# Turning the probabilities of the banded heads: four TensorE transposes into PSUM, or one transposing DMA per pair inside SBUF

## The chip, the cores and the metric

The kernel runs on one core of a Trainium2 chip. The metric is the device time of one execution in microseconds; three executions of the kernel before were timed and their median is used. A separate execution was profiled, and every row shown below comes from that one.

## What is computed

One decoder layer for 2048 tokens of width 1024. The input is normalised and projected once; the projection feeds two attention mixers of eight heads each (head width 64). Mixer A, "FoX", is causal attention with a cumulative forget-gate bias. Mixer B is a banded attention: each query sees itself and the 127 keys before it, plus one learned logit per head (the sink) in the softmax. Both outputs are gated, concatenated, projected out, normalised and added to the input. The change is in mixer B:

```python
def sliding_window_sink_attention(q, k, v, sinks):        # blocks of 128 queries
    ...
    s = jnp.einsum('bnqhgd,bnshd->bnhgqs', qb, kk, ...) * (d ** -0.5)   # keys: previous block and own block
    ...
    s = jnp.where(mask[None, :, None, None], s, -jnp.inf)               # the band of 128 keys
    sink = jnp.broadcast_to(sinks..., s.shape[:-1] + (1,))
    p = jax.nn.softmax(jnp.concatenate([s, sink], axis=-1), axis=-1)[..., :-1]
    out = jnp.einsum('bnhgqs,bnshd->bnqhgd', p.astype(vv.dtype), vv)
    return out.reshape(B, S, SWA_Q_HEADS * d)
```

## The kernel before

The layer runs in four stages: a prologue (conditioning vectors, the first weights, the normalised input turned to `hT`), the banded stage, the FoX stage and the output projection. Numbers that need more than half precision are kept as two 16-bit parts, a high one and the rest ("high" and "low"), and every product is made of three matmuls: high by high, high by low, low by high.

**The banded stage** is a list of 32 windows. Window n does the parts of one *pair*: two blocks of 128 queries times two heads, so four 128x128 probability tiles with queries on partitions. The matrix work of other projections (`proj_units`, `value_units`, lines L351 and L369) is cut into units and poured between these parts by `fill`, so that TensorE always has something to do. A pair goes through these steps, each a method of the class `Pair`:

- `scores` (L889): twelve matmuls into one PSUM tile `pss`, at the end of the window before its own.
- `maxima` (L896 to L904), VectorE: the band mask is written into `pss`, the sink logit into one column, the row maximum is taken, and L904 makes the bias `b_nb` of the exponential.
- `exps` (L911), ScalarE: four exponentials from `pss` to `sm_` in SBUF, 32-bit, with their row sums in `b_rs`.
- `turn` (L914 on), one window later: TensorE transposes the four tiles of `sm_` into the PSUM tile `pxb` (L918). A step later ScalarE copies `pxb` to 16 bits (`fold[:, 0]`, L927), VectorE subtracts that copy from `pxb` (`fold[:, 1]`, L928) and takes the reciprocal of the row sums (L930), and GpSimd cuts the band's two triangles out of `fold` with four affine selects (L932, L934) into `ptb`. There is one buffer `fold`.
- `pv` (L946), another window later: 24 matmuls of `ptb` with the values, then VectorE scales (L952), and `o_store` (L285 to L295) splits the result and stores it to DRAM `o_d`.

**What sets the order.** The program is recorded in the order in which each engine then runs; nothing is reordered. `after(n, f)` puts a function off by n ticks, and `tick` runs those that are due. A window holds four ticks, one for each quarter of its filling units:

```python
            tick()
            if n:
                wd.maxima()
            fill(part[0])
            if n:
                windows[n - 1].turn()
            tick()
            if n:
                wd.exps()
            fill(part[1])
            tick()
            if n > 1:
                windows[n - 2].pv()
```

after which follow `fill(part[2])`, `tick()`, `fill(part[3])`, the `scores` of the next window, and one load of `w_out` rows for a sum of squares (`wsq`, L1183 and L1179).

**Other users of the same queues in this stage.** SyncE's DMA queue issues the four quarter copies `qs<-qf` of each rotary projection (L751), which VectorE reads five ticks later (L764, L765) and whose end is L768 and L758, and the `wsq` loads. GpSimd issues, in its own order between the selects, weight loads (L221), the gate path's stores (L394), the stores to `o_d`, and for each weight a column of 128 maxima written to DRAM (`mx_d`, L230, 4 bytes a row) and read back as a row (`mxr`, L235), on which VectorE waits before it scales that weight (L246 to L253). PSUM has three banks `bk` for the filling units; a bank is free again when ScalarE and VectorE have read it (L749 and L754, L396 and L392, L375 and L379).

In the output stage, from 981 us on, `load` reads `o_d` with DMAs that transpose on the way (L1483, 128 rows of 1024 16-bit numbers each). They are the only transposing DMAs of the kernel before.

Of the kernel before, what the change touches and what calls it, by code (L numbers as in the profile page):

```python
# [10 lines left out]
F32 = mybir.dt.float32  # L11
F16 = mybir.dt.float16
# [3 lines left out]
AF = mybir.ActivationFunctionType  # L16
ALU = mybir.AluOpType
AX = mybir.AxisListType

P = 128  # L20
# [4 lines left out]
CH = 512  # L25
# [18 lines left out]
def hybrid_layer(  # L44
# [17 lines left out]
    V, A, G, PE, SP = nc.vector, nc.scalar, nc.gpsimd, nc.tensor, nc.sync  # L62
# [5 lines left out]
    PSUM = bass.MemoryType.PSUM  # L68
# [14 lines left out]
    def sm(n, tag):  # L83
        return small.tile([P, n], F32, tag=tag, name=tag)
# [71 lines left out]
    ident = const.tile([P, P], F32, name="ident")  # L156
# [45 lines left out]
    def after(n, f):  # L202
        late.append([n, f])

    def tick():
        now = [f for n, f in late if n <= 1]
        late[:] = [[n - 1, f] for n, f in late if n > 1]
        for f in now:
            f()
# [221 lines left out]
    def turn(ci, k, px=None):  # L431

        px = px or ps_x.tile([P, CH], F32, tag="x", name="px")
        for u in range(4):
            PE.transpose(px[:, u * P:(u + 1) * P], xt[ci * 4 + u][:, k * P:(k + 1) * P], ident[:])
        hf = hst.tile([P, CH], F32, tag="hf", name="hf")
        hi, lo = hT[ci][:, 0, k, :], hT[ci][:, 1, k, :]

        def scaled():
            for dst in ([hi] if k % 2 == 0 else []) + [hf[:]]:  # L440
                A.activation(dst, px[:], AF.Identity, scale=Gp[:, k:k + 1], bias=Shp[:, k:k + 1])

        def split():
            if k % 2:
                V.tensor_copy(hi, hf[:])
            V.tensor_tensor(lo, hf[:], hi, op=ALU.subtract)

        return scaled, split

    def turn_x(ci, k):  # L450
        scaled, split = turn(ci, k)
        after(1, scaled)
        after(2, split)
# [10 lines left out]
    st = start.enter_context(tc.tile_pool(name="start", bufs=1, reuse_waits="tile"))  # L464
    wad = start.enter_context(tc.tile_pool(name="wad", bufs=8, reuse_waits="tile"))
    with tc.manual_schedule():
# [172 lines left out]
        w_low("kb", 0, 1)  # L639
        w_low("vb", 0, 1)  # L640
        turned = [turn(0, k) for k in range(5)]
        squares(1)
        shf0 = col8("shf0")
# [9 lines left out]

        PE.transpose(bk[0][0:1, 0:P], bmx[:], ident[:])
        turned += [turn(0, k, bk[k - 4]) for k in (5, 6)]
        bm = st.tile([1, 1], F32, name="bm")
        V.tensor_reduce(bm[:], bk[0][0:1, 0:P], axis=AX.X, op=ALU.max)
# [66 lines left out]
    def swa_pool(name, bufs, **kw):  # L724
        return swa.enter_context(tc.tile_pool(name=name, bufs=bufs, reuse_waits="tile", **kw))
# [3 lines left out]
    stp = swa_pool("stp", 2)  # L729
# [143 lines left out]
    class Pair:  # L873
# [32 lines left out]
        def exps(self):  # L906
# [3 lines left out]
            for n in range(4):  # L910
                A.activation(self.sm_[:, n], self.s4[:, n // 2, n % 2], AF.Exp, scale=scl[key][:],  # L911
                             bias=self.nb[:, n:n + 1], accum_out=self.rs[:, n:n + 1])

        def turn(self):  # L914

            px = ps_t.tile([P, 4, P], F32, tag="t", name="pxb")
            for n in range(4):
                PE.transpose(px[:, n, :], self.sm_[:, n, 1:P + 1], ident[:])  # L918
            even = (8 * self.j + self.i // 2) % 2 == 0
            self.ptt = [ptp.tile([P, 2, 4, P], F16, tag=f"pt{b}", name="ptb") if even else  # L920
                        stp.tile([P, 2, CH], F16, tag="st", name="ptb") for b in range(2)]
            ptt = [t[:].rearrange("p a (n c) -> p a n c", n=4) if not even else t[:] for t in self.ptt]
            self.ptt = ptt
            fold = ptp.tile([P, 2, 4, P], F16, tag="fo", name="fold")

            def split():
                A.activation(fold[:, 0], px[:], AF.Copy)  # L927
                V.tensor_tensor(fold[:, 1], px[:], fold[:, 0], op=ALU.subtract)  # L928
                self.rinv = sm(4, "b_ri")
                V.reciprocal(self.rinv[:], self.rs[:])  # L930
                for n in range(2):
                    G.affine_select(ptt[0][:, n], fold[:, n], [[0, 4], [-1, P]], ALU.is_ge, 0.0,  # L932
                                    base=-1, channel_multiplier=1)
                    G.affine_select(ptt[1][:, n], fold[:, n], [[0, 4], [1, P]], ALU.is_ge, 0.0,  # L934
                                    base=0, channel_multiplier=-1)

            after(1, split)

        def pv(self):
            j, i = self.j, self.i  # L940
# [178 lines left out]
    def fill(n, each=None):  # L1119

        for _ in range(n):
            for f in events.pop(pos[0], []):
                f()
            punits[pos[0]]()
            pos[0] += 1
            if each:
                each()
# [9 lines left out]
    with swa_order:  # L1137
        fill(N_PRO - 4, tick2)
        psx.close()
        sws = swa_pool("sws", 2)  # L1140
        ptp = swa_pool("ptp", 1)
        ps_s = swa_pool("ps_s", 1, space=PSUM)
        ps_t = swa_pool("ps_t", 1, space=PSUM)
        ps_pv = swa_pool("ps_pv", 1, space=PSUM)
        wsp = swa_pool("wsp", 2)
        wss, wst = sm(16, "a_m"), sm(2, "wst")
        wsq = {}
        base = N_PRO
        NW = len(windows)
        windows[0].scores()  # L1150
        windows[0].maxima()
        fill(2, tick2)
        windows[0].exps()
        fill(2, tick2)
        for n, wd in enumerate(windows):
            goal = base + (N_SWA - base) * (n + 1) // NW
            todo = goal - pos[0]
            part = [todo * (m + 1) // 4 - todo * m // 4 for m in range(4)]
# [13 lines that stand above are left out]
            fill(part[2])  # L1172
            tick()
            fill(part[3])
            if n + 1 < NW:
                windows[n + 1].scores()

            if n:
                A.activation(wsq[n - 1][:], wsq[n - 1][:], AF.Square, accum_out=wss[:, (n - 1) % 16:(n - 1) % 16 + 1])  # L1179
            if n == 16:  # L1180
                V.tensor_reduce(wst[:, 0:1], wss[:], axis=AX.X, op=ALU.add)
            wsq[n] = wsp.tile([P, 2 * P], F32, tag="wsq", name="wsq")
            SP.dma_start(wsq[n][:], w_out0[n // 4 * P:(n // 4 + 1) * P, n % 4 * 2 * P:(n % 4 + 1) * 2 * P])  # L1183
        tick()
        fill(5)
        windows[NW - 1].turn()
        tick()
        fill(5)
        windows[NW - 2].pv()
        tick()  # L1190
        fill(6)
        windows[NW - 1].pv()
        tick()
        tick()
        A.activation(wsq[NW - 1][:], wsq[NW - 1][:], AF.Square, accum_out=wss[:, 15:16])
        V.tensor_reduce(wst[:, 1:2], wss[:], axis=AX.X, op=ALU.add)
        wsum = sm(1, "w_mx2")
        V.tensor_reduce(wsum[:], wst[:], axis=AX.X, op=ALU.add)
# [16 lines left out]
    stp = foxl.enter_context(tc.tile_pool(name="stpa", bufs=3, reuse_waits="tile"))  # L1215
# [115 lines left out]
    class Step:  # L1331
# [30 lines left out]
        def low(self):  # L1362
            V.tensor_tensor(self.ph[:, 1, :self.w], self.p32[:, :self.w], self.ph[:, 0, :self.w], op=ALU.subtract)  # L1363
# [271 lines left out]
    with tc.manual_schedule():  # L1635
# [35 lines left out]
        for s, stp_ in enumerate(steps):  # L1671
# [11 lines left out]
            a = b = 0  # L1683
# [100 lines left out]
```

## Time and profile before

| | |
|---|---|
| median of three runs | 1157.67 us (1157.06 to 1159.82) |
| the profiled execution | 1157.8 us, of which the profile's span is 1156.1 |
| TensorE matmul, busy | 1116.8 us, 97% of the span |
| VectorE, busy | 930.5 us, 80% |
| ScalarE, busy | 661.4 us, 57% |
| GpSimd, busy | 207.5 us, 18% |
| banded stage, first exponentials to last `pv` | 155.8 to 413.7 us |

The profile names a group of instructions by its line in the kernel, the engine, and what it writes and reads (`out<-in`). In a row of a group, "x32" is the number of instructions, the number behind it the mean in nanoseconds, and the part behind the last bar the idle time of that engine just before them and who ended it. PE is TensorE's matmul and PEld its weight load, DVE is VectorE, ACT ScalarE, POOL GpSimd, and SPq SyncE's DMA queue. The matmuls are pipelined, so what one costs is read from the starts of its neighbours and not from its own length.

### The profile page before, as it was taken

Reading aid. Unit: us, or ns where it says so; the run is one execution under the profiler, and the core shown is the slowest. Engines: PE = TensorE matmul, PEld = TensorE weight load, DVE = VectorE, ACT = ScalarE, POOL = GpSimd, SP = SyncE. Lnnn points to the kernel's source line nnn. Section 1 sums busy time; section 2 is a strip of 40 time slices with the busy share of each in tenths; the row PEclk is TensorE's granted clock in tenths of the full one; section 3 lists DMA queues with packets and bytes.
Section 4 is the critical chain, followed back from the end, with each engine's and each line's share of the span. In section 5 each row is a group of like instructions: output and inputs, shape, how many; then the busy total and the mean of one; then the engine's idle time right before and its main releaser. Section 6 shows DMA issues by size and latency. Waiting matters only on the chain. (4 is left out here: it accounts for less than half of the span.)

```text
span 1156.1 us, 25291 instructions
## 1 busy us (share of the span) xinstructions
PE 1116.8 (97%) x9869; PEld 656.3 (57%) x9869; DVE 930.5 (80%) x2137; ACT 661.4 (57%) x1150; POOL 207.5 (18%) x332
## 2 busy tenths in 40 slices
PE   5899999999999999999999999999999999999997
PEld 2475544577765866555555555555555555544444
DVE  7877468987888568788988899888888887878885
ACT  2876344654555421666757666666776778534332
POOL 1122134554556530010010110001000000000000
PEclk9899999999999999999999999999999999999999
DMA  9943355433243232442344342123311337686743
GB/s 333 336 116 72 87 78 96 97 63 90 52 92 88 58 87 58 73 108 29 80 64 87 84 67 70 38 49 76 45 43 34 91 101 206 140 225 197 199 135 109
DMA packets 123476, 120.10 MB, mean 104 GB/s; under 512 B 64948, under 2 KB 100828, under 8 KB 123356
## 3 DMA queue, kind: packets, MB, share of 16 engines
q1 hardware_dynamic: 112088, 85.69, 27.6%
q0 software_dynamic: 10832, 32.50, 13.5%
q8 instruction: 77, 1.26, 0.6%
q14 instruction: 43, 0.35, 0.1%
q10 hardware_dynamic: 436, 0.28, 0.1%
HBM read 64.75 MB, written 25.18 MB: 78 GB/s over the span
## 5 line engine op out<-in xcount | busy, mean ns | idle before, releaser
L1356 ACT ACTIVATE p<-sta,lift,scl_qk 128x1024 f32<-128x1024 f32 (+2 forms) x160 | 172.0, 1075 | 131.6 <-PE sta L1350 82.6
L351 PE MATMUL bk<-hT,wh_qk 128*128 128x512 f16 x768 | 194.7, 378 | 0.0
L1363 DVE TENSOR_TENSOR pha<-p,pha 128x1024 f16<-128x1024 f32 (+2 forms) x160 | 169.1, 1057 | 0.2 <-ACT pha L1360 0.2
L1303 DVE TENSOR_REDUCE a_m<-bk 128x1 f32<-128x512 f32 x192 | 130.4, 686 | 45.8 <-PE bk L1300 44.8
L1576 PE MATMUL bk<-wohl,oz 128*128 128x512 f16 x744 | 165.3, 379 | 1.1 <-DVE oz L1525 0.7
L1360 ACT ACTIVATE pha<-p 128x1024 f16<-128x1024 f32 (+2 forms) x160 | 148.1, 926 | 5.9 <-PE poa L1376 1.2
L1576 PEld LDWEIGHTS <-oz 128*128 128x128 f16 x744 | 71.9, 99 | 82.8 <-DVE oz L1525 1.8
L1376 PE MATMUL poa<-vt,pha 128*128 128x65 f16 x1088 | 116.1, 192 | 1.4 <-DVE pha L1363 1.2
L1373 PE MATMUL poa<-vt,pha 128*128 128x65 f16 x1088 | 116.6, 193 | 0.8 <-DVE ona L1382 0.7
L1375 PE MATMUL poa<-vt,pha 128*128 128x64 f16 x1088 | 116.6, 194 | 0.0
L351 PEld LDWEIGHTS <-wh_qk 128*128 128x128 f16 x768 | 72.1, 97 | 74.4 <-issue 2.1
L1349 PE MATMUL sta<-T 128*128 128x512 f16 (+1 forms) x320 | 110.9, 346 | 2.8 <-ACT p L1356 2.7
L1300 PE MATMUL bk<-T 66*128 66x512 f16 (+2 forms) x320 | 109.7, 348 | 2.4 <-DVE a_m L1303 1.9
L1373 PEld LDWEIGHTS <-pha 128*128 128x128 f16 x1088 | 101.5, 96 | 15.5 <-DVE ona L1382 1.9
L1350 PE MATMUL sta<-T 69*128 69x512 f16 (+1 forms) x320 | 109.8, 348 | 0.0
L1375 PEld LDWEIGHTS <-pha 128*128 128x128 f16 x1088 | 100.9, 97 | 11.4
L1376 PEld LDWEIGHTS <-pha 128*128 128x128 f16 x1088 | 100.8, 99 | 1.8 <-DVE pha L1363 1.7
L351 PE MATMUL bk<-hT,wh_za 128*128 128x512 f16 x384 | 99.7, 378 | 0.0
L369 PE MATMUL bk<-wh_va,hT 128*128 128x256 f16 x768 | 91.9, 273 | 0.0
L351 PE MATMUL bk<-hT,wh_zb 128*128 128x512 f16 x384 | 91.6, 379 | 0.2 <-DVE qc L754 0.2
L351 PE MATMUL bk<-hT,wh_qb 128*128 128x512 f16 x384 | 91.2, 379 | 0.0
L369 PEld LDWEIGHTS <-hT 128*128 128x128 f16 x768 | 73.3, 98 | 12.2 <-issue 2.1
(459 smaller groups left out, 1919.7 us busy)
## 6 DMA issues: line engine op xcount, KB each, us to landing
hT<-in_x_dram SPq DMA_DIRECT2D x20, 512.0 KB
wa<-in_w_ada_dram SPq DMA_DIRECT2D x16, 512.0 KB
z_d<-tz POOLq DMA_DIRECT2D x32, 256.0 KB, 3.0
T<-z_d SPq DMA_DIRECT2D x16, 512.0 KB
T<-stq SPq DMA_DIRECT2D x62, 128.0 KB
out_dram<-hT SPq DMA_DIRECT2D x15, 512.0 KB
xt<-in_x_dram SPq DMA_DIRECT2D x12, 512.0 KB
qs<-qf SPq DMA_DIRECT2D x80, 64.0 KB
```

The lines of the kernel that those rows point to most:

```text
L351: PE.matmul(ps, whl[:, a, k, :], hT[ci][:, b, k, :], start=(k == 0 and n == 0), stop=(k == KT - 1 and n == 2))
L369: PE.matmul(ps[:, (u % 2) * 2 * P:(u % 2 + 1) * 2 * P], hT[ci][:, a, k, u * P:(u + 1) * P], wv[p][:, b, k, :], start=(k == 0 and n == 0), ...
L1303: V.tensor_reduce(m3[:, u, pc:pc + 1], mx[:, :w], axis=AX.X, op=ALU.max)
L1349: PE.matmul(self.st[:, o:o + w], T[:, 3, kb_], T[:, 1, qc], start=True, stop=False)
L1350: PE.matmul(self.st[:, o:o + w], T[0:XR, 2, kb_], T[0:XR, 0, qc], start=False, stop=not diag)
L1356: A.activation(self.p32[:, :self.w], self.st[:, :self.w], AF.Exp, scale=scl[f"qk{self.hd}"][:], bias=lift[:])
L1360: A.activation(self.ph[:, 0, :self.w], self.p32[:, :self.w], AF.Copy)
L1363: V.tensor_tensor(self.ph[:, 1, :self.w], self.p32[:, :self.w], self.ph[:, 0, :self.w], op=ALU.subtract)
L1373: PE.matmul(po[:, u, :], ph[:, 0, pq], vt[:, b, hd, 0:65], start=(self.first and n == 0 and u == 0), stop=False)
L1375: PE.matmul(po[:, u, 0:64], ph[:, 0, pq], vt[:, b, hd, 65:VW], start=False, stop=False)
L1376: PE.matmul(po[:, u, :], ph[:, 1, pq], vt[:, b, hd, 0:65], start=False, stop=(self.last and n == len(self.blocks) - 1))
L1576: PE.matmul(py, self.hl[:, i, k, :], w_slot(8 * j + k)[:, cc], start=(k == 0 and m_ == 0), stop=(k == KT - 1 and m_ == 2))
```

## The change

The split into two 16-bit parts is made first, with queries still on partitions, and a DMA then turns both parts at once. Behind the four exponentials ScalarE copies `sm_` to 16 bits (`fq[:, 0]`, L915). One tick later VectorE subtracts that copy from `sm_` (`fq[:, 1]`, L919), SyncE's queue issues one transposing DMA from `fq` to `fold` (L920, 128 rows of 1024 16-bit numbers), and VectorE takes the reciprocal (L923). `turn` keeps the four affine selects alone (L935, L937). The TensorE transposes and the PSUM tile `pxb` are gone. `fq` and `fold` have one buffer each, and `sm_` has one in place of two. From there on line numbers are one higher than before (L952 becomes L953).

```diff
@@ exps / turn
+            fq = ptp.tile([P, 2, 4, P], F16, tag="fq", name="fq")
+            A.activation(fq[:, 0], self.sm_[:, :, 1:P + 1], AF.Copy)
+            self.fold = ptp.tile([P, 2, 4, P], F16, tag="fo", name="fold")
+
+            def low():
+                V.tensor_tensor(fq[:, 1], self.sm_[:, :, 1:P + 1], fq[:, 0], op=ALU.subtract)
+                SP.dma_start_transpose(self.fold[:].rearrange("p a n c -> p (a n) c"),
+                                       fq[:].rearrange("p a n c -> p (a n c)"))
+                self.rinv = sm(4, "b_ri")
+                V.reciprocal(self.rinv[:], self.rs[:])
+
+            after(1, low)
+
         def turn(self):
-            px = ps_t.tile([P, 4, P], F32, tag="t", name="pxb")
-            for n in range(4):
-                PE.transpose(px[:, n, :], self.sm_[:, n, 1:P + 1], ident[:])
             even = (8 * self.j + self.i // 2) % 2 == 0
...
-            fold = ptp.tile([P, 2, 4, P], F16, tag="fo", name="fold")
-            def split():
-                A.activation(fold[:, 0], px[:], AF.Copy)
-                V.tensor_tensor(fold[:, 1], px[:], fold[:, 0], op=ALU.subtract)
-                self.rinv = sm(4, "b_ri")
-                V.reciprocal(self.rinv[:], self.rs[:])
-                for n in range(2):
-                    G.affine_select(ptt[0][:, n], fold[:, n], ...)
-                    G.affine_select(ptt[1][:, n], fold[:, n], ...)
-            after(1, split)
+            for n in range(2):
+                G.affine_select(ptt[0][:, n], self.fold[:, n], ...)
+                G.affine_select(ptt[1][:, n], self.fold[:, n], ...)
@@ pools of the stage
-        sws = swa_pool("sws", 2)
+        sws = swa_pool("sws", 1)
-        ps_t = swa_pool("ps_t", 1, space=PSUM)
```

**VectorE, around one pair** (the first pair of the second head group, a quarter into the stage). Before, from the bias of this pair's exponentials (L904) on; `fold` and `b_ri` are of the pair before:

```order
L904 TENSOR_SCALAR b_nb<-b_m,nscl_qb_2236 128x4
L291 TENSOR_TENSOR oh<-on,oh 128x2x128
L928 TENSOR_TENSOR fold<-pxb,fold 128x512
L930 RECIPROCAL b_ri<-b_rs 128x4
L227 TENSOR_REDUCE w_mx<-wr_qb_2688 128x1
L758 TENSOR_TENSOR stb<-qc,stb 128x512
L754 SCALAR_TENSOR_TENSOR qc<-bk_138,cosT 128x512
L952 TENSOR_TENSOR on<-pob,b_ri 128x256
```

Now, at the same place; `fq` and `b_ri` are of this pair itself:

```order
L904 TENSOR_SCALAR b_nb<-b_m,nscl_qb_2227 128x4
L291 TENSOR_TENSOR oh<-on,oh 128x2x128
L227 TENSOR_REDUCE w_mx<-wr_qb_2674 128x1
L758 TENSOR_TENSOR stb<-qc,stb 128x512
L754 SCALAR_TENSOR_TENSOR qc<-bk_138,cosT 128x512
L919 TENSOR_TENSOR fq<-sm__2809,fq 128x512
L923 RECIPROCAL b_ri<-b_rs 128x4
L953 TENSOR_TENSOR on<-pob,b_ri 128x256
```

The subtraction has moved a tick down in VectorE's row of work, but it belongs to the pair whose bias stands just above it, and no longer to the pair before.

**SyncE's DMA queue, over three windows.** Before, between two sets of rotary copies:

```order
L751 DMA qs<-qf 32x512 x4
L1183 DMA wsq<-in_w_out_dram 128x256 x3
L751 DMA qs<-qf 32x512 x4
L1183 DMA wsq<-in_w_out_dram 128x256 x2
L751 DMA qs<-qf 32x512 x4
```

Now, the same three `wsq` loads and the copies on either side:

```order
L751 DMA qs<-qf 32x512 x4
L920 DMA_TRANSPOSE fold<-fq 128x8x128
L1183 DMA wsq<-in_w_out_dram 128x256
L920 DMA_TRANSPOSE fold<-fq 128x8x128
L1183 DMA wsq<-in_w_out_dram 128x256
L920 DMA_TRANSPOSE fold<-fq 128x8x128
L1183 DMA wsq<-in_w_out_dram 128x256
L751 DMA qs<-qf 32x512 x4
```

One transposing DMA per window has come in. Each waits for VectorE's subtraction of its own pair, and for GpSimd's selects of the pair before, since both pairs use the one `fold`; what is behind it in the queue waits with it.

More of the change, by code (lines that the diff above doesn't have):

```diff
@@ L912, in exps @@
                              bias=self.nb[:, n:n + 1], accum_out=self.rs[:, n:n + 1])
-        def turn(self):
-            px = ps_t.tile([P, 4, P], F32, tag="t", name="pxb")
-            for n in range(4):
[L918 to L923, printed above, removed]
-            fold = ptp.tile([P, 2, 4, P], F16, tag="fo", name="fold")
-            def split():
-                A.activation(fold[:, 0], px[:], AF.Copy)
-                V.tensor_tensor(fold[:, 1], px[:], fold[:, 0], op=ALU.subtract)
+            fq = ptp.tile([P, 2, 4, P], F16, tag="fq", name="fq")
@@ L929, in split @@
+            A.activation(fq[:, 0], self.sm_[:, :, 1:P + 1], AF.Copy)
[4 more added lines that the diff above has]
+                                       fq[:].rearrange("p a n c -> p (a n c)"))
                 self.rinv = sm(4, "b_ri")
                 V.reciprocal(self.rinv[:], self.rs[:])
-                for n in range(2):
[L932 to L935, printed above, removed]
@@ L937, in turn @@
-            after(1, split)
+            after(1, low)
+        def turn(self):
+            even = (8 * self.j + self.i // 2) % 2 == 0
+            ptt = [ptp.tile([P, 2, 4, P], F16, tag=f"pt{b}", name="ptb")[:] if even else
+                   stp.tile([P, 2, CH], F16, tag="st", name="ptb")[:].rearrange("p a (n c) -> p a n c", n=4)
+                   for b in range(2)]
+            self.ptt = ptt
+            for n in range(2):
+                G.affine_select(ptt[0][:, n], self.fold[:, n], [[0, 4], [-1, P]], ALU.is_ge, 0.0,
+                                base=-1, channel_multiplier=1)
+                G.affine_select(ptt[1][:, n], self.fold[:, n], [[0, 4], [1, P]], ALU.is_ge, 0.0,
+                                base=0, channel_multiplier=-1)
```

## The prediction

> **What bounds the kernel now.** I read the page first, then the busy time by stretches of the banded stage, then the groups and the timeline inside it.
>
> ```profile
> span 1156.1 us, 25291 instructions
> 160.00:240.00 80.00, 77.66 (x664) 44.10 (x662) 68.92 (x158) 43.53 (x135) 42.76 (x64) 1.00 0.46 90
> 240.00:320.00 80.00, 80.00 (x836) 57.86 (x836) 64.22 (x149) 43.15 (x140) 41.27 (x58) 1.00 0.26 66
> 320.00:400.00 80.00, 79.88 (x801) 53.53 (x799) 61.02 (x132) 44.44 (x148) 46.50 (x67) 1.00 0.35 85
> L904 DVE TENSOR_SCALAR b_nb<-b_m,nscl_qb x32: 229/229/298, 155.5 to 396.2; 128x4 f32<-128x4 f32 x32
> ```
>
> The columns of the stretches are PE, PEld, DVE, ACT and POOL busy, the granted clock, the DMA share and GB/s. TensorE is busy in 237.5 of 240 us: the stage is paced by TensorE, and time taken out of TensorE's row is gained as long as nothing else falls behind. The bias L904 comes once per window, so a window lasts (396.2 - 155.5) / 31 = 7.76 us. VectorE is busy in 194.2 of the 240 us, so 6.28 us of each window: it has 1.48 us to spare on average, and that is the number on which this case hangs. In the first stretch TensorE already lost 2.3 us; the group and the timeline say to whom:
>
> ```profile
> L889 PE MATMUL pss<-kst,stb 64*128 64x256 f16 (+1 forms) x384 | 25.9, 267 | 2.5 <-ACT sm__2471 L911 1.9 <-ACT sm__2836 L911 0.4
> 199.05 0.23 DVE L904 TENSOR_SCALAR b_nb<-b_m,nscl_qb 128x4 f32<-128x4 f32 x1
> 199.32 0.46 ACT L911 ACTIVATE sm__2471<-pss,b_nb,scl_qb 128x129 f32<-128x129 f32 x1 [3.11 <-DVE b_nb L904]
> 200.64 0.46 ACT L911 ACTIVATE sm__2471<-pss,b_nb,scl_qb 128x129 f32<-128x129 f32 x1
> ```
>
> The next scores may not overwrite `pss` before the exponentials have read it, the exponentials wait for VectorE's bias, and VectorE was late. So the way in which VectorE's lateness reaches TensorE is known: through L904, L911 and L889.
>
> **TensorE's part of the change.**
>
> ```profile
> 202.01 1.47 PE L351 MATMUL bk<-hT,wh_qb 128*128 128x512 f16 x6
> 203.31 0.60 PE L918 MATMUL pxb<-ident,sm__2471 128*128 128x128 f32 x4
> 203.75 1.46 PE L351 MATMUL bk<-hT,wh_qb 128*128 128x512 f16 x6
> ```
>
> Four transposes hold the matmul row from 203.31 to 203.75, 0.44 us, on the path that paces the stage. Thirty-two pairs: -14.1 us if TensorE stays the pace, and a window of 7.32 us. Nothing is added to TensorE. This is the most the change can gain.
>
> **ScalarE.** The copy moves from PSUM and one window later to SBUF and right behind the exponentials.
>
> ```profile
> L927 ACT ACTIVATE fold<-pxb 128x512 f16<-128x512 f32 x32 | 19.0, 594 | 39.9 <-PE pxb L918 30.5 <-issue 5.0 <-POOL ptb L934 4.4
> L768 ACT ACTIVATE stb<-qc 128x512 f16<-128x512 f32 x15 | 9.5, 631 | 24.1 <-DVE qc L765 24.1
> ```
>
> The nearest row from SBUF takes 0.63 us against 0.59, 1.2 us more in 32, on an engine that is busy in 131 of 240 us: nothing. A wait of 39.9 us before the old copy goes too, but it was ScalarE's idle time.
>
> **VectorE: a wait comes in.** The number of instructions is the same. The place is not: the subtraction L919 now needs the copy that follows this pair's own exponentials. From the end of L904 (199.28) to the end of the fourth exponential (201.10) and of a copy of 0.63 us it is 201.73 at the earliest, and 0.1 more with the accumulators read out, so 2.55 us. What VectorE finds in its row between L904 and L919 fills that time, the rest is a stall, and everything behind it waits: L953, the evacuations L754 and L392 that free banks for TensorE, and the next pair's maxima. In the order shown above L291, L227, L758 and L754 stand between, 2.7 us, and there is no stall. At the next pair only L291 and L392 stand there, 0.9 us, and the stall is 1.6. Rows follow each other about 0.08 us closer than they are long:
>
> ```profile
> 196.20 0.68 DVE L758 TENSOR_TENSOR stb<-qc,stb 128x512 f16<-128x512 f32 x1
> 196.80 0.68 DVE L754 SCALAR_TENSOR_TENSOR qc<-bk,cosT 128x512 f32<-128x512 f32 x1
> ```
>
> Pricing VectorE's rows of 31 windows that way, each by its group's duration less that overlap, I estimate 34.6 us of stalls in all, 1.1 us a window. With 6.28 us of work that is 7.4 us against a pace of 7.32: VectorE becomes as slow as TensorE on average. But the windows are uneven, their work runs from 3.7 to 9.1 us, and what a light window leaves over is no help to the heavy one before it. By the same count eleven windows pass 7.32 us, by 12.7 us in sum; before, without the stall and against 7.76, four passed by 2.9 us. So +9.8 us. The bounds are 0, if each stall falls into VectorE's 1.48 us of idle time, and 34.6, if all of it reaches TensorE.
>
> **GpSimd and the port.** The four selects stay, 128 instructions, and run at another moment, as soon as the DMA has landed.
>
> ```profile
> 190.92 0.65 POOL L932 TENSOR_SCALAR_AFFINE_SELECT ptb<-fold 128x512 f16<-128x512 f16 x1
> 190.96 2.92 DVE L765 TENSOR_TENSOR qc<-qc,qs 128x512 f32<-128x512 f32 x1
> 192.69 0.63 POOL L934 TENSOR_SCALAR_AFFINE_SELECT ptb<-fold 128x512 f16<-128x512 f16 x1
> L928 DVE TENSOR_TENSOR fold<-pxb,fold 128x512 f16<-128x512 f32 x32 | 21.9, 683 | 1.3 <-ACT fold L927 1.3
> L764 DVE TENSOR_TENSOR qs<-qs,sinT 128x512 f32<-128x512 f32 x15 | 15.8, 1051 | 0.7 <-DMA qs<-qf 0.4 <-issue 0.3
> ```
>
> A VectorE addition with both inputs in SBUF took 2.92 us while four selects ran, and ended 0.56 us behind them; L764, of the same kind, has a mean of 1.05. The old subtraction, with one input in PSUM, has 0.683 and was never held. The new one reads both from SBUF and can be held. The ends are -5.5 us (L764's 15 x 0.37 gone, the selects fall elsewhere) and +20.5 (32 x 0.64, one select each time). I take 0: the selects come 4 to 7 us behind their subtraction, before the next one. [...]
>
> **The DMA.** No transfer within SBUF that transposes is in the trace. The nearest rows are the transposing loads of the same shape from DRAM; one of them began in a quiet moment (the last columns are clock, DMA share, GB/s):
>
> ```profile
> L1483 SPq DMA_TRANSPOSE T<-o_d x24: 1244/1480/3466, 981.3 to 1098.6; - x24
> 994.12 1.24 SPq L1483 DMA_TRANSPOSE T<-o_d  x1
> 994.50:995.00 0.50, 1.00 0.00 0
> 995.00:995.50 0.50, 1.00 0.05 12
> 996.00:996.50 0.50, 1.00 1.11 251
> 996.50:997.00 0.50, 1.00 0.52 103
> ```
>
> Issued at 994.12, moving from about 995.4, done before 997: 2.9 us, and I take 3.1 with the signal. Copy 0.63, subtraction 0.69, DMA 3.1 and four selects (2.6) end 7.0 us behind the exponentials; `pv` wants them some 15 us behind. So on average the DMA hides behind a window of matmuls. If that cover goes, the single `fq` stops ScalarE at the next copy, which comes 7.32 us behind the last one: 7.32 - 0.69 - 3.1 leaves 2.9 to 3.5 us of slack. The issue itself takes 1.24 to 1.48 us of SyncE's queue, 40 to 47 us in 32; the rotary copies behind it start that much later, and VectorE met them late once in the stage (0.4 us above). For that I take 0, at most 15 x 1.48 = 22 us.
>
> What breaks the cover is already there:
>
> ```profile
> DMA to landing us min/median/max: 7.4/8.5/10.5
> L235 POOL DMA_DIRECT2D mxr<-mx_d x10 | 5.6, 562 | 19.5 <-DMA mx_d<-w_mx 19.3 <-issue 0.2
> 179.33 2.42 SPq L751 DMA_DIRECT2D qs<-qf  x4
> 179.48 0.56 POOL L230 DMA_DIRECT2D mx_d<-w_mx  x1 [1.39 <-DVE w_mx L227]
> 189.78 0.58 POOL L235 DMA_DIRECT2D mxr<-mx_d  x1 [2.01 <-DMA mx_d<-w_mx]
> 190.23 0.69 DVE L764 TENSOR_TENSOR qs<-qs,sinT 128x512 f32<-128x512 f32 x1 [0.39 <-DMA qs<-qf]
> ```
>
> The first row is the landing of L230, the column of maxima. While one was under way from 179.48 to 189.78, the rotary copies issued by 181.75 did not land either until 190.2. Ten such stores in the stage, 8.5 us each, cover 85 of 258 us, so about ten of the 32 transposing DMAs are held, by anything from 0 to 8.5 us. Held by more than 2.9, ScalarE stops: on average (8.5 - 2.9)^2 / (2 x 8.5) = 1.8 us, 18 us in ten. The three banks give TensorE something to do for part of that; I take a half less a little, +8 us, with ends 0 and 18.
>
> **The sum.** 1157.8 (the profiled execution, 1.7 us outside its span, 0.1 over the median of the runs) - 14.1 + 9.8 + 8 = 1161.5; I say 1162. A measurement of this kernel can tell 0.3%, 3.5 us, from no change.
>
> **Rivals.** (1) *The gain stays.* VectorE's stalls fall into its idle time and the selects and banks carry the held DMAs: -14.1 with 2 to 3 us of losses, 1146. For it speaks the spare 1.48 us against a stall of 1.1; against it the uneven windows, and L889, which waited already. It decides if VectorE's work and stall in the heavy windows stay under 7.32 us. 0.25. (2) *The loop over `fold`.* A DMA waits for the selects of the pair before, and these for their DMA: DMA plus 2.9 us (four selects, one held). From a DMA of 4.4 us on, this is longer than 7.32 and paces every window. With 3.47 us of issue, the longest in the row of L1483, and 2.1 behind it, it is 8.5 us: 31 x (8.5 - 7.76) = +23, 1181. For it speaks that reading 256-byte pieces out of SBUF is not in the trace; against it the 2.9 us above. 0.17. [...] (3) *Gain and loss meet* within 3.5 us: 1158. 0.15.
>
> My forecast, slower by some 4 us with a range of its own from 1155 to 1170, has 0.43. Of that the part below 1161.3 belongs to "same" with most of rival 3: same 0.17, faster 0.25, slower 0.58. The range from 1147 to 1184 leaves out half of rival 1 and a part of rival 2 beyond 1184.
>
> **What would show it.** Right: in the rows of after, no L918; VectorE idle before L919 with ScalarE's `fq` as its releaser, near 35 us in sum; idle time before L889 put down to L911 well over 2.5 us; ScalarE idle before L915 with the DMA of `fold` as releaser, about ten times. The light windows at 7.3 us and a few at 9. Wrong: VectorE's wait at L919 there but no idle TensorE (rival 1); idle time before every L915 or L920 by the selects, and even windows above 8 us (rival 2); L919 with a mean far over 0.7 us, which would mean that the port was mis-sized.

## The result: 27 us slower

The changed kernel takes 1184.66 us (median of four executions, 1183.49 to 1194.21) against 1157.57 beside it: a ratio of 1.0249, 95% interval 1.0219 to 1.0278. The forecast was 1162 in a range from 1147 to 1184, so the time lies just above the range. The direction held, the size did not: +27 in place of +4. The profiled execution took 1183.9 us.

The page's first line and the busy time by stretches of the profile after, in the columns of the prediction:

```profile
span 1182.1 us, 25164 instructions
160.00:240.00 80.00, 67.50 (x546) 34.92 (x545) 62.02 (x143) 39.37 (x119) 35.75 (x53) 0.98 0.52 110
240.00:320.00 80.00, 68.20 (x688) 46.48 (x687) 52.24 (x115) 36.37 (x118) 38.00 (x52) 0.99 0.54 92
320.00:400.00 80.00, 71.59 (x658) 42.52 (x658) 61.97 (x143) 43.48 (x134) 42.61 (x61) 0.97 0.53 104
```

TensorE was full and no longer is (207.3 of 240 us, 237.5 before), its granted clock fell below 1.00, and VectorE is not busier either (176.2, 194.2 before). The stage, from the first scores to the last `pv`, has grown from 261.1 to 284.3 us. Where it went stands in VectorE's waits. First the kernel before, the stage as one stretch:

```profile
152.50:414.00 261.50, 259.04 (x2501) 171.57 (x2500) 204.08 (x463) 137.45 (x437) 137.76 (x198) 1.00 0.36 79
```

and what VectorE waited for in it (us in total, times, longest; the first seven rows):

```profile
DVE pss L897 <- PE pss L889: 14.7, 10, 3.7
DVE w_mx L246 <- DMA mxr<-mx_d: 12.4, 4, 6.6
DVE tz L392 <- ACT tz L396: 5.4, 3, 2.6
DVE pss L896 <- PE pss L889: 4.9, 3, 2.0
DVE wh_va L273 <- ACT wh_va L267: 3.9, 2, 2.0
DVE vt L379 <- ACT vt L375: 2.7, 3, 1.5
DVE on L952 <- PE pob L946: 2.7, 3, 1.3
```

The same two views of the kernel after, the first seven rows again:

```profile
153.00:438.00 285.00, 251.79 (x2374) 159.73 (x2373) 200.75 (x457) 141.28 (x437) 137.19 (x197) 0.98 0.51 100
```

```profile
DVE fq L919 <- ACT fq L915: 55.5, 26, 5.2
DVE w_mx L246 <- DMA mxr<-mx_d: 9.6, 2, 6.6
DVE qs L764 <- DMA qs<-qf: 6.7, 1, 6.7
DVE stb L758 <- ACT stb L768: 3.0, 1, 3.0
DVE pss L896 <- PE pss L889: 2.0, 1, 2.0
DVE w_mx L227 <- DMA wr_qb<-in_w_in_dram: 1.0, 1, 1.0
DVE pss L897 <- PE pss L889: 1.0, 1, 1.0
```

This pair of lists is the reading of the case. Before, 22.3 us of VectorE's idle time were waits for TensorE (L896, L897, L952): VectorE was early, and TensorE set the pace. After, 3.0 us of that is left and 55.5 us wait at L919. VectorE is hardly ever early any more: the stage is its work plus its other waits, and TensorE follows. Seen from TensorE, 14.1 us of transposes less, 30.7 us more idle (33.2 against 2.5, summed from the gaps in its row) and 2% of the clock over 285 us, 5.7, make +22. The stage of the profiled executions grew by 23.2 us, and 2 us more came behind it.

The longest window (14.2 us from its scores to the next) shows how it happens. From the timelines of SyncE's queue, GpSimd, VectorE, ScalarE and TensorE:

```profile
301.69 2.99 SPq L751 DMA_DIRECT2D qs<-qf  x4
308.31 1.29 SPq L920 DMA_TRANSPOSE fold<-fq  x1
...
301.77 0.56 POOL L230 DMA_DIRECT2D mx_d<-w_mx  x1 [0.78 <-DVE w_mx L227]
308.18 0.55 POOL L230 DMA_DIRECT2D mx_d<-w_mx  x1
320.16 0.63 POOL L935 TENSOR_SCALAR_AFFINE_SELECT ptb<-fold 128x512 f16<-128x512 f16 x1 [6.61 <-DMA fold<-fq]
...
316.01 0.69 DVE L764 TENSOR_TENSOR qs<-qs,sinT 128x512 f32<-128x512 f32 x1 [6.70 <-DMA qs<-qf]
...
319.34 0.46 ACT L911 ACTIVATE sm__4020<-pss,b_nb,scl_qb 128x129 f32<-128x129 f32 x1 [0.65 <-DVE b_nb L904]
...
321.26 1.46 PE L889 MATMUL pss<-kst,stb 64*128 64x256 f16 x12 [6.85 <-ACT sm__4020 L911]
```

Two stores of a column of maxima are under way (301.77 and 308.18). What waits for the rotary copies issued at 301.69 goes on at 316.0, and what waits for the transposing DMA of 308.31 at 320.1 to 320.2. VectorE stands still for 6.70 us, its bias is late, the exponentials are late, and TensorE waits 6.85 us before the next scores. In all, six of the 32 transposing DMAs took 6.6 to 11.9 us from issue to the first select, and each of the six had such a store under way beside it.

### The profile page after: what moved, and what is told of

Read it like the earlier page. It is cut to its first block, busy times and chain, and to the rows that moved or that the text cites. A ratio compares the mean times of both kernels' runs of the same rounds, so it can differ in the third digit from the quotient of the medians.

```text
span 1182.1 us, 25164 instructions
## 1 busy us (share of the span) xinstructions
PE 1109.9 (94%) x9741; PEld 644.2 (54%) x9741; DVE 928.3 (79%) x2137; ACT 664.5 (56%) x1150; POOL 208.4 (18%) x332
## 3 DMA queue, kind: packets, MB, share of 16 engines
q8 instruction: 76, 1.25, 0.5%
## 5 line engine op out<-in xcount | busy, mean ns | idle before, releaser
L1373 PEld LDWEIGHTS <-pha 128*128 128x128 f16 x1088 | 101.5, 96 | 15.5 <-DVE ona L1382 1.9
L1375 PEld LDWEIGHTS <-pha 128*128 128x128 f16 x1088 | 100.9, 97 | 11.4
```

Of the source, the lines that this page charges most:

```text
L1373: PE.matmul(po[:, u, :], ph[:, 0, pq], vt[:, b, hd, 0:65], start=(self.first and n == 0 and u == 0), stop=False)
L1375: PE.matmul(po[:, u, 0:64], ph[:, 0, pq], vt[:, b, hd, 65:VW], start=False, stop=False)
```

## Experiments

All changes are to the kernel after (names with "before": to the kernel before). In all runs named three, and in before_dma, new_place, mid and old_place_dma, the rotary results have three buffers in place of four (`abp 3`), to make room. In the table, "stage" runs from the first scores to the last `pv` of the profiled execution; the next columns are VectorE's busy time in it, its waits at the subtraction, and its waits for TensorE, each summed from the trace.

| kernel | median us | ratio to before (95%) | stage | VectorE busy | wait at subtraction | wait for TensorE |
|---|---|---|---|---|---|---|
| before | 1156.8 to 1157.6 | | 261.1 | 204.0 | 1.3 | 22.3 |
| after | 1184.7 | 1.0249 (1.0219 to 1.0278) | 284.3 | 201.0 | 55.5 | 3.0 |
| three | 1171.0 | 1.0124 (1.0105 to 1.0143) | 273.3 | 203.9 | 38.6 | 5.0 |
| three_late | 1173.9 | 1.0147 (1.0132 to 1.0162) | 273.6 | 203.2 | 24.7 | 6.6 |
| three_turn | 1172.7 | 1.0115 (1.0081 to 1.0150) | 274.9 | 215.3 | 40.2 | 4.6 |
| three_late_turn | 1170.0 | 1.0112 (1.0097 to 1.0127) | 272.1 | 210.9 | 25.2 | 4.7 |
| three_later_turn | 1183.1 | 1.0219 (1.0197 to 1.0241) | 281.7 | 206.1 | 5.5 | 14.5 |
| no_dma | 1171.7 | 1.0136 (1.0118 to 1.0153) | 274.4 | 214.2 | 39.2 | 8.7 |
| no_dma_later | 1166.6 | 1.0079 (1.0064 to 1.0094) | 268.6 | 208.8 | 6.6 | 11.0 |
| new_place | 1171.5 | 1.0125 (1.0108 to 1.0142) | 273.8 | 217.6 | 38.9 | 4.9 |
| before_sbuf | 1150.3 | 0.9930 (0.9913 to 0.9946) | 253.8 | 201.0 | 1.4 | 14.4 |
| before_one_turn | 1153.3 | 0.9956 (0.9941 to 0.9971) | 253.9 | 202.5 | 0.7 | 14.3 |
| before_dma | 1160.9 | 1.0037 (1.0018 to 1.0056) | 263.8 | 204.3 | 1.6 | 25.1 |
| three_no_sel | 1162.3 | 1.0048 (1.0031 to 1.0065) | 267.4 | 188.1 | 40.6 | 14.7 |
| before_no_sel | 1158.9 | 1.0012 (1.0002 to 1.0022) | 261.4 | 188.0 | 2.0 | 37.3 |
| after_no_mxd | 1162.0 | 1.0050 (1.0035 to 1.0065) | 272.1 | 202.5 | 48.8 | 11.2 |
| before_no_mxd | 1155.3 | 0.9989 (0.9980 to 0.9998) | 258.9 | 204.8 | 1.6 | 27.7 |
| three_no_mxd | 1163.4 | 1.0064 (1.0047 to 1.0081) | 262.6 | 204.0 | 36.9 | 11.3 |
| mid | 1217.5 | 1.0533 (1.0501 to 1.0565) | 316.1 | 210.1 | 34.5 | 39.0 |
| old_place_dma | 1214.8 | 1.0496 (1.0477 to 1.0516) | 312.7 | 203.0 | 89.5 | 8.5 |

The profiled execution of after_no_mxd (1170.0) lies 8 us above its median, that of three_no_mxd (1159.0) 4 us below; for these two the medians count.

### Buffers, place, DMA

**three**

```diff
-fq: tag="fq", 1 buffer; fold: tag="fo", 1 buffer; abp 4
+fq and fold: tag="fo", bufs=3, in rotation; abp 3
```

> The changed kernel with three buffers that fq and fold share in rotation, in place of one each (the rotary results get three buffers in place of four to make room); order of all engines as in the changed kernel. Loop over the single buffers: ScalarE's 16.9 us before L915 on the DMA and SyncE's waits for the selects go, and 15 us or more of the 27 come back: 1165 to 1170. Stall of VectorE at its place: the wait before L919 falls only by those 16.9 us, from 55.5 to about 39, and the rest still reaches TensorE: 1175 to 1182.

1171.0: 13.7 us back, just short of what the buffers were to give. ScalarE no longer waits for a DMA before L915. VectorE's two longest waits in it:

```profile
DVE fq L919 <- ACT fq L915: 38.6, 25, 2.7
DVE w_mx L246 <- DMA mxr<-mx_d: 15.5, 3, 11.0
```

The wait at L919 fell by 16.9 us, as much as ScalarE waited for the DMA in the kernel after; 38.6 us are the subtraction's own stall, as expected, and half of the loss is still there.

**three_late**

```diff
-            after(1, low)
+            after(2, low)
```

> As three, and the subtraction, its DMA and the reciprocal one tick later in VectorE's row (after(2) for after(1)). Stall of VectorE at its place: the wait before L919 falls under 15 us and TensorE's 14.1 us show: 1148 to 1160. Loop over the single buffers: no more than three gives, within 4 us of it. DMA traffic or held DMAs: also within 4 us of three.

1173.9: the wait at L919 fell to 24.7 us, not under 15, and nothing was gained. VectorE's waits for DMAs rose to 23.4 us and its other waits for ScalarE to 10.7 (19.7 and 1.4 in three).

**no_dma**

```diff
+            self.fold = fq                      # fq with two buffers
-                SP.dma_start_transpose(self.fold, fq)
```

> The changed kernel without the DMA: fq has two buffers and the selects read it directly, so the tiles are not turned (that part is left out). Stall of VectorE at its place: the wait for this pair's exponentials and copy stays, 35 to 40 us before L919, and the time stays at 1165 to 1175. Latency or traffic of the DMA: the gain of 14 us shows, 1145 to 1150.

1171.7, as the stall has it: without any DMA the loss is that of three. One thing was new. The bias, 128x4 elements, in the groups of this kernel:

```profile
L904 DVE TENSOR_SCALAR b_nb<-b_m,nscl_qb 128x4 f32<-128x4 f32 x32 | 18.1, 566 | 1.1
```

566 ns in the mean in place of 232, since the selects, released early, often ran beside it: one bias that began at 194.88, with four selects from 194.87 on, took 1.83 us. "The port", in the prediction and in the expectations, is the author's name for this: a VectorE instruction takes longer while selects run. The runs show how much longer, not what holds it.

**before_dma**

```diff
+            after(1, lambda: SP.dma_start_transpose(fd[:], hT[0][:, 0, 0:2, :]...))   # shortened; 32 times
```

> The kernel before plus 32 transposing DMAs of the same size at the places of the new ones, from a finished tile of hT into a tile that nobody reads (rotary results in three buffers). DMA traffic: the 1.25 us of SyncE's queue and the packets delay the rotary copies, weight loads and the row of maxima, 1165 to 1178. Stall of VectorE or loop over the buffers: within 4 us of the kernel before, 1157 to 1161.

+3.7 us. The traffic and the 1.25 us (median) of each issue on SyncE's queue cost little where nobody waits for the result; VectorE still waits 25.1 us for TensorE.

### Moving the selects and the subtraction

```diff
 three_turn:        turn(n-1) behind pv(n-2) of the window, not behind its first filling
 three_late_turn:   the same, and after(2, low)
 three_later_turn:  the same, and after(3, low)
 no_dma_later:      as three_later_turn, without the DMA (fold = fq, two buffers)
```

> As three, and the selects of a pair (turn) later in GpSimd's row: behind pv of the window, a tick and a quarter of the filling later; the subtraction stays one tick behind the exponentials. GpSimd held by its wait for the DMA (70.3 us in three), so that the row of maxima is read late and VectorE waits at L246 (15.5 us in three): that wait falls under 8 us and 5 to 8 us come back, 1163 to 1166. VectorE's stall at L919 alone: 38 to 40 us stay there and the time stays at 1169 to 1172.

> As three_turn, and the subtraction, its DMA and the reciprocal two ticks behind the exponentials. Both waits of VectorE count: L919 falls to about 25 us, L246 under 12 us, and the time to 1154 to 1162. The traffic of the DMAs, or the latency: no more than 3 us off three_turn.

> As three_turn, and the subtraction, its DMA and the reciprocal three ticks behind the exponentials, just ahead of the next pair's maxima. VectorE's waits are the cause: none is left at L919 (under 3 us), TensorE is idle under 5 us in the stage, its clock stays at 1.00, and the 14 us of the transposes show less the 4 that the DMAs cost beside the kernel before: 1145 to 1151, faster than both. If the DMA's traffic or GpSimd's selects on VectorE's port are the cause, it stays above 1158.

> As three_later_turn, but without the DMA: two buffers fq, and the selects read fq, so the tiles are not turned (that part is left out). VectorE's waits are the cause: 1143 to 1147, and the difference to three_later_turn is what the DMA itself costs, 0 to 5 us. If GpSimd's selects on VectorE's port are the cause (the bias L904 took 0.566 us in no_dma against 0.232 before), it stays above 1155.

1172.7, 1170.0, 1183.1 and 1166.6. The theory that the stall at L919 alone, or with the wait at L246, is the cause fell here: three_later_turn has 5.5 us of stall and loses as much as the kernel after. The waits were not taken away but moved. In three_turn and three_late_turn VectorE's busy time rose by 11 and 7 us, the subtraction now meeting the selects (it takes 1.21 and 1.05 us in the mean, 0.76 in three); in three_later_turn its waits for DMAs and ScalarE are 24.0 and 26.4 us. In no_dma_later 26.1 us are waits for ScalarE. Both kernels stay above the mark that their expectations set for the selects, but VectorE's busy time in them, 206.1 and 208.8 us, is only 2 and 5 us above that of before, so what the selects hold up does not explain their loss alone.

### What TensorE's time is worth, and the selects

```diff
 before_one_turn:  for n in range(1) in place of range(4) at L918 (rest of pxb filled once)
 before_sbuf:      no transposes; px = self.sm_[:, :, 1:P + 1]
 three_no_sel:     no affine selects, pv reads fold (fq two buffers, fold three)
 before_no_sel:    no affine selects, pv reads fold (two buffers)
```

> The kernel before with one of the four TensorE transposes of a pair (the other three tiles of pxb are filled once and stay): all instructions of the other engines at their old places. TensorE sets the pace: three quarters of 14.1 us are gained, 1146 to 1149. VectorE's row and its waits set the pace as soon as TensorE is a little faster: under 4 us gained, 1154 to 1157.

> The kernel before without the TensorE transposes: the copy and the subtraction stand where they stood, one window after the exponentials, and read sm_ in SBUF in place of pxb (the tiles are not turned: that part is left out). It has neither the stall at L919 nor a DMA. If the place of the split behind its own exponentials is the cause: 1143 to 1148. If the second SBUF input of the subtraction is the cause (the port with GpSimd's selects), or TensorE's time is worth nothing: 1155 or more.

> The changed kernel without the affine selects (the band's triangles are left out; pv reads fold), with two buffers fq and three fold. The selects behind the DMA are the cause, by the port and by GpSimd's queue held for the DMA: 1144 to 1152. VectorE's stall for its own exponentials is the cause: it stays at 1162 to 1170.

> The control of three_no_sel: the kernel before without the selects (pv reads fold, two buffers). TensorE paces it: 1155 to 1158, nothing gained but the 2 us of idle time of TensorE.

before_one_turn gains 4.0 of the 10.6 us it takes off TensorE, before_sbuf 7.0 of 14.1, in between the two theories both times. So taking the transposes away gained 7 us, even with the split (the copy and the subtraction) at its old place and no DMA. The stretch of the stage for the two kernels without selects, three_no_sel first:

```profile
153.50:421.00 267.50, 250.26 (x2372) 159.30 (x2371) 188.15 (x462) 141.60 (x437) 48.26 (x70) 0.98 0.66 109
```

```profile
153.50:415.00 261.50, 258.85 (x2500) 171.63 (x2499) 188.01 (x462) 137.70 (x437) 48.27 (x70) 1.00 0.38 80
```

Without the selects VectorE is busy for 16 us less in both (the third busy time: 188 against 204), since its instructions are no longer held by them. In the kernel before, leaving them out gains nothing (+1.6); in three it gains 8.6 us. The edit also frees GpSimd's queue, and `fq` and `fold` have five buffers in place of three: VectorE's wait for the row of maxima (L246) is 8.3 us, 15.5 in three. So how much of the 8.6 is VectorE's shorter work is not shown. The same relief gains or does not, depending on who sets the pace.

### Place and stores of the maxima

**new_place**

```diff
 as no_dma, sm_ with two buffers, and in turn():
+            after(1, select)                    # the four selects at their old tick
```

> The changed kernel without the DMA, fq with two buffers, sm_ with two, and the selects at their old tick of the next window, reading fq (the tiles are not turned: that part is left out). Beside the kernel with the split at its old place and no transposes (1150.3) only the copy and the subtraction have moved, behind their own exponentials. VectorE's stall there is the cause of the rest: 1160 to 1166. The moment of the selects was it (they met the bias in no_dma): 1149 to 1154.

1171.5, worse than the stall alone was to give. Against before_sbuf (1150.3), which has neither DMA nor transposes either, the copy and the subtraction have moved (and a few buffers differ): +21.2. The two stages, before_sbuf first:

```profile
155.00:409.00 254.00, 247.30 (x2372) 157.84 (x2372) 201.09 (x463) 138.76 (x437) 143.07 (x198) 0.99 0.36 80
```

```profile
153.00:427.00 274.00, 251.07 (x2372) 159.66 (x2372) 217.68 (x463) 141.54 (x437) 140.72 (x198) 0.99 0.31 74
```

By the table VectorE is busy 16.6 us longer with as many instructions (463; that the selects hold it more often is the author's estimate) and waits 37.5 us more at L919, against 9.5 us less for TensorE, 15.0 less elsewhere for ScalarE and 8.7 less for DMAs. That leaves 20.9 us, and the stage grew by 20.0.

**after_no_mxd, before_no_mxd**

```diff
-        G.dma_start(md[:], mx[:])
+        if len(kaps_seen) <= 3: G.dma_start(md[:], mx[:])
```

> The changed kernel without the stores of the column of maxima behind the first three (L230; the rows read back are those of earlier weights, so the scales of the later ones are not their own). DMAs held by these stores: 7 of the 32 were late by 3 to 8 us; without them 6 to 12 us come back beyond what the control gains, 1172 to 1178. Not held: within 3 us of the changed kernel.

> The control: the kernel before without the same stores. TensorE paces it and VectorE met the row of maxima late for 12 us that were its idle time: 1154 to 1158.

1162.0: 22.7 us come back, 21 beyond the 1.7 of the control, where 6 to 12 were expected. **three_no_mxd** completes the square (three buffers and no stores):

> The changed kernel with three shared buffers for fq and fold, and without the stores of the column of maxima behind the first three. If those stores cost only by holding the transposing DMA, and that only through the single buffers, it stays with three at 1169 to 1172, and VectorE's wait at L919 stays near 38 us. If they cost because VectorE, with no slack left, waits for the row of maxima itself (L246, 19.7 us of DMA waits in three), 8 to 12 us come back beyond the 2 of the control: 1158 to 1162.

| median us | with the stores | without |
|---|---|---|
| single buffers | 1184.7 | 1162.0 |
| three buffers | 1171.0 | 1163.4 |

Without the stores, single buffers cost nothing that these runs can show (1162.0 and 1163.4, ranges 1161.3 to 1170.0 and 1159.0 to 1166.3). So the single buffers cost their 14 us only beside these stores. The stores could act in two ways: they hold the transposing DMA, or GpSimd stops before it reads the row back (L235) and its selects come late. The trace of the kernel after speaks for the first: behind each of those stops that the trace puts down to a store inside the stage (they end at 154.58, 191.11, 313.00, 359.60 and 375.38) the next select still waited 2.1 to 6.6 us for its DMA. But the stores are not all that can hold it: in the profiled execution of after_no_mxd one transposing DMA, issued at 338.57, released its selects only at 352.35, with no such store under way, and ScalarE waited 7.8 us for it. What held it there is not known. In three the stores still cost 7.6, 6 more than in the control, nearer to VectorE's own wait for the row of maxima than to no cost at all: of those waits one is left. VectorE's two longest waits in three_no_mxd, whose line numbers are one higher:

```profile
DVE fq L920 <- ACT fq L916: 36.9, 25, 2.7
DVE w_mx L247 <- DMA mxr<-mx_d: 3.9, 1, 3.9
```

### Two versions meant to be faster

**mid** and **old_place_dma**

```diff
 mid:            copy, low and DMA in after(4); sm_ two buffers; turn at the end of the window, pv a tick later
 old_place_dma:  copy, low and DMA in after(5); sm_ two buffers; turn(n-2), pv(n-3)
```

> The change with the copy, the subtraction and the DMA four ticks behind the exponentials, that is behind the next pair's maxima and ahead of its exponentials, sm_ with two buffers, the selects at the end of the window and pv a tick later; rotary results in three buffers. If the place and the waits are the cause, what is left is 7 us gained for the transposes less the 4 of the DMAs: 1152 to 1157. If the DMA, held or not, costs more than that wherever it stands: 1162 or more.

> The transposing DMA with the copy and the subtraction at their old tick of the next window, the selects at the start of the window after it and pv at the start of the one after that; sm_ with two buffers, fq and fold with one each, rotary results in three. VectorE waits no longer at L919 (under 5 us): 1150 for the split at its old place without transposes plus 4 for the DMAs, 1152 to 1157, no slower than the kernel before. If the DMA costs what it costs wherever it stands: 1165 or more.

1217.5 and 1214.8, some 50 us above even the bound from which the second expectation counts ("or more"). They do not test the place. With the split later, less time is left between the DMA and the next copy into the one `fq`, and the waits fit a loop that sets the pace: copy, subtraction, DMA, selects, next DMA, over single buffers. Waits in old_place_dma, from 156 to 440 us:

```profile
POOL ptb L935 <- DMA fold<-fq: 109.6, 27, 9.2
DVE fq L919 <- ACT fq L918: 77.9, 24, 7.5
ACT fq L918 <- DMA fold<-fq: 36.4, 13, 5.9
PE pob L947 <- POOL ptb L935: 26.5, 15, 3.7
```

TensorE now waits for the selects before `pv` (L947), which it did for 0.3 us in the kernel after. No kernel that does the whole computation beat the kernel before.

## Why the prediction was right and wrong

**Path: right.** VectorE is late at L904, the exponentials are late, the scores are late: TensorE's idle time before L889 is 23.9 us (2.5 before). Another 8.7 us lie before `pv` (L947), nearly all of it put down to VectorE's L953.

**TensorE's term, -14.1: right as work, wrong as gain.** 7.0 us of it show in before_sbuf.

**The stall, 34.6 us: right. The spare time it was priced against: the step that failed.** 38.6 us in three and 36.9 in three_no_mxd are the stall without ScalarE's waits for the DMA. It was set against "1.48 us to spare", VectorE's whole idle time, and so came to +9.8. The full -14.1, and the nothing for other lateness of VectorE, rest on the same spare time. But idle time is not slack. Of 57.2 us in the stage, 14.5 were waits for DMAs, which stay, and 22.3 were waits for TensorE, 0.70 a window; those for ScalarE, 13.6, mostly went too. TensorE's 14.1 us come out of the same slack. What remained, 8 to 22 us, was to carry 35 to 39. In three TensorE's idle time grew by 20.9 us and not by 9.8. Gain and stall together were -4.3 in the forecast; measured are +13.7 in three, and +8.1 in three_no_mxd beside before_no_mxd (1163.4 against 1155.3), the traffic of the DMAs included.

What the stall costs by itself is not settled. In new_place it is 21.2 us, with the stores there and with 16.6 us more of VectorE's busy time. In three_no_mxd it is 11.4 if the 7.0 of before_sbuf and the 3.7 of before_dma simply add up with it. By that second reckoning the +9.8 was not far off, and the same mistake shows in TensorE's full -14.1, in the half taken for the held DMAs and in the late row of maxima.

**The selects beside VectorE, 0: right in sum, wrong in its argument.** VectorE's busy time in the stage is 204.0 before and 201.0 after. But "the selects come before the next subtraction" is false: one landing releases both, as the rows of GpSimd and ScalarE show,

```profile
207.17 0.62 POOL L935 TENSOR_SCALAR_AFFINE_SELECT ptb<-fold 128x512 f16<-128x512 f16 x1 [7.36 <-DMA fold<-fq]
...
207.09 0.63 ACT L915 ACTIVATE fq<-sm__2453 128x512 f16<-128x512 f32 x1 [2.20 <-DMA fold<-fq]
```

and the subtraction then runs against them. From the rows of L919, one alone and one beside selects:

```profile
L919 DVE TENSOR_TENSOR fq<-sm__1893,fq x1: 693/693/693, 159.1 to 159.1; 128x512 f16<-128x512 f32 x1
L919 DVE TENSOR_TENSOR fq<-sm__2453,fq x1: 1173/1173/1173, 207.8 to 207.8; 128x512 f16<-128x512 f32 x1
```

13 of the 32 took over 1 us, the mean is 0.93; the old subtraction took 0.67 to 0.69 in all 32. Other instructions were held less in return, L764 for one: 1.05 us in the mean before, 0.78 after.

**The DMA, 3.1 us: right when undisturbed.** One issue and the select that it released:

```profile
397.43 1.28 SPq L920 DMA_TRANSPOSE fold<-fq  x1
...
400.63 0.66 POOL L935 TENSOR_SCALAR_AFFINE_SELECT ptb<-fold 128x512 f16<-128x512 f16 x1 [1.02 <-DMA fold<-fq]
```

So 3.2 us, the shortest of the 32; over all of them the median from issue to the first select is 4.4. The queue and the traffic, taken as 0, are 3.7 (before_dma).

**The held DMAs, +8 (0 to 18): right mechanism, too small.** ScalarE waits for the DMA before L915 eleven times for 16.9 us; the forecast had "about ten" and 18:

```profile
ACT fq L915 <- DMA fold<-fq: 16.9, 11, 3.5
POOL ptb L935 <- DMA fold<-fq: 84.5, 28, 7.4
```

That the count fits is in part luck. Four of the eleven (10.4 us) follow a DMA with a store of maxima beside it. Six of the other seven follow a DMA that was issued only when the selects of the pair before had ended, with no store under way: the loop of rival 2. What the waits cost, by the square, is 14 to 15 us. "A half less a little" assumed that TensorE's banks carry a part of each stop, which takes slack again.

**Not in the sum:** what the stores cost beyond the single buffers, about 6 us (7.6 in three, less the 1.7 of the control). The row of maxima was late before too, for 12.4 us, but then at next to no cost.

**The rivals.** Rival 2 gave 1181 by the loop over `fold`, close in time but only in part in kind. Its loop was there: the median of 4.4 us is just the limit that it named, and 18 of the 32 DMAs were issued within 0.1 us of the end of the selects before. But the windows are uneven, from 6.7 to 14.2 us from scores to scores. The light ones ran at 7.2 to 7.5, as forecast (7.3); over 9 us there were eleven, not "a few". And without the stores the same loop (16 of 32 DMAs in after_no_mxd) costs nothing beside three buffers. The waits for the selects in mid and old_place_dma are of its kind.

**Open.** The parts overlap (13.7 and 22.7 us come back singly, 21.3 together), so 27 us can't be split exactly. Why no_dma_later, with 6.6 us of stall and no DMA, still loses 9.5 us is only described: VectorE busy 7.8 us longer and waiting 11.1 us more for ScalarE than in before_sbuf.

## What to carry to other kernels

Before a wait is put into an engine's row, split that engine's idle time by what ends it: in this case only the waits for the engine that set the pace were slack, and the faster that engine got, the less there was of it. Once the slack is gone, costs that were always there (16 us by which VectorE's work is longer beside the selects, a late row of maxima) begin to count, and taking any one of them away looks like the cause. A single buffer was cheap here as long as the transfer behind it was not held; look for what else in flight can hold it.

## What the runs showed of the hardware

TensorE's granted clock fell to a half behind some of its gaps. From the stretches of 2 us of the kernel after, around the long wait above (PE, PEld, DVE, ACT and POOL busy, clock, DMA share, GB/s):

```profile
314.00:316.00 2.00, 0.41 (x4) 0.12 (x2) 0.00 (x0) 0.00 (x0) 0.00 (x0) 1.00 0.69 102
316.00:318.00 2.00, 0.00 (x0) 0.00 (x0) 1.96 (x3) 0.64 (x3) 0.00 (x0) 1.00 0.81 133
318.00:320.00 2.00, 0.00 (x0) 0.10 (x1) 1.90 (x6) 1.35 (x5) 0.00 (x0) 0.58 0.02 2
320.00:322.00 2.00, 0.74 (x8) 0.62 (x9) 0.25 (x2) 1.97 (x8) 1.84 (x4) 0.50 0.00 0
322.00:324.00 2.00, 2.00 (x15) 1.19 (x12) 1.94 (x6) 0.75 (x3) 2.00 (x3) 0.50 0.00 0
324.00:326.00 2.00, 2.00 (x15) 1.58 (x14) 1.85 (x6) 1.42 (x2) 1.07 (x2) 0.72 0.82 153
326.00:328.00 2.00, 2.00 (x38) 1.86 (x37) 1.63 (x5) 1.78 (x8) 0.00 (x0) 1.00 0.77 217
```

A wait of 6.85 us is followed by some 4 us of matmuls at half clock (321.26 to about 325.1, from the 0.72 of the stretch in which it ends), so this stall cost more than its length: the twelve scores behind it took 1.46 us, those at 307.08, at a clock of 1.00, took 0.83. The length of the gap alone does not tell what follows: behind a gap of 2.41 us (202.53 to 204.94) the stretches of 1 us show 0.50 from 206 to 209, while behind one of 2.90 us (231.96 to 234.86) they stay at 1.00.
